# A 16-expert MoE layer with two token sets: the context products issued in runs of four k tiles instead of two

## The chip, the core and the metric

The kernel runs on one core of a Trainium2 chip. A core has TensorE (PE in the profile, with its weight loads shown as PEld), VectorE (DVE), ScalarE (ACT), GpSimd (POOL), SyncE (SP, which here only issues transfers) and sixteen DMA engines. The metric is device time in microseconds; the number quoted for a kernel is the median of several executions. Everything that is read from the trace comes from one further profiled execution, with times counted from the start of its span.

## The reference, cut to what matters

The model has two layers over 1024 latent tokens and 256 context tokens with 1024 channels. Each layer is a token mixer followed by an expert-choice mixture of experts: each of 16 experts picks its own tokens, 128 latent ones and, in layer 0 only, 32 context ones, and applies a gated two-layer network to them.

```python
def _ec_moe(h, router, w1, w3, w2):
    bsz, n_tok, d = h.shape
    cap = EC_CAPACITY * n_tok // N_EXPERTS
    aff = jax.nn.softmax(jnp.einsum('btd,de->bte', h, router).astype(F32), axis=-1)
    gate, idx = lax.top_k(jnp.swapaxes(aff, 1, 2), cap)
    xe = jax.vmap(lambda hb, ib: hb[ib])(h, idx)
    hid = jax.nn.silu(jnp.einsum('becd,edf->becf', xe, w1)) * jnp.einsum('becd,edf->becf', xe, w3)
    ye = jnp.einsum('becf,efd->becd', hid, w2) * gate[..., None].astype(h.dtype)
    ...
for i in range(DEPTH):
    ...
    x_lat = x_lat + mod_l[5] * _ec_moe(...)
    if i < DEPTH - 1:
        x_ctx = x_ctx + mod_c[5] * _ec_moe(...)
```

The weights `w1`, `w3` and `w2` of an expert are 1024 x 1024 each, in 32-bit floats, and both token sets use the same ones.

## The kernel before

`Moe` works through the sixteen experts of a layer. In layer 0 it has two token sets. The three matrices of an expert are cut into eight k tiles of 128 rows each. `tiles` loads two k tiles at a time (1 MB) into a `raw` buffer, of which layer 0 has eight, and makes of each k tile two operands: `uhi`, the value rounded to a short significand, on ACT (line 1184, inside `split_hl`), and `ulo`, the rest, on DVE (line 1185). Layer 0 has six buffers for each of these.

The products of the 128 latent tokens use these operands: for a k tile of a matrix there are three products (high by high, high by low, low by high) with two halves of 512 columns, six matmuls over the whole 128 x 128 array (lines 1573 in `up`, 1624 in `down`). The products of the 32 context tokens use `raw` itself in full 32-bit floats. They use 32 columns of the array, so four of them, for four blocks of columns of the weights, stand side by side in four column groups and write to the four 32-partition bands of one PSUM bank (lines 1579 in `up`, with 512 columns each, and 1630 in `down`, with 256). In the records each of these 32-bit matmuls shows as two MATMUL instructions.

`up` computes the hidden activations from `w1` and `w3`, `down` the output from `w2`. Both collect the k tiles in `raws` and issue the context products of the last `CG` of them in one go, behind the latent products of the last one. This text calls that a run. With `CG = 2` there is a run behind k tiles 1, 3, 5 and 7: four in each `up` and four in each `down`. A run of `up` has 16 MATMUL instructions in the records (two k tiles, four groups, two each), and so has one of `down`.

`run` orders the work: `up` of expert e, halfway through it (behind k tile 3) `turn` of the expert before, which transposes its hidden activations, and `operands` of the next expert, which transposes its gathered rows; then `down` of the expert before. Every engine works through its own instructions in a fixed order, which the tile framework's planner lays down when the program is built; mostly it is the order of the code, with small exchanges.

SP issues the loads of `raw` (line 1512) in order. A load waits until its buffer is free, that is until both splits and the context products of the buffer's earlier content are done. The order of the buffers is: for k tiles 0 and 1 `w1`, then `w3`, and so on, eight loads for an `up`, then four for a `down`.

Layer 1 has no context tokens in its MoE, other buffer counts, and no runs.

Of the kernel before, what the change touches and what calls it, by code (L numbers as in the profile page):

```python
# [17 lines left out]
DRAM = bass.MemoryType.DRAM  # L18

D = 1024  # L20
NCTX = 256
NLAT = 1024
T = NCTX + NLAT
# [8 lines left out]
def step_of(m):  # L32
    """Step at which direction 1 meets chunk m, and the chunk of a step."""
    return 3 - m if m < 4 else 23 - m
# [6 lines left out]
def rows_ap(t, off, rows, cols):  # L41
    """rows x cols view of a contiguous DRAM tensor, from element `off`."""
    return bass.AP(tensor=t.tensor, offset=t.offset + off, ap=[[cols, rows], [1, cols]])
# [12 lines left out]
def log_exp_table(K):  # L56
    """Loads the activation table that serves Ln and Exp together."""
    K.table = K.tc.keep_in_program_order(K.nc.scalar.preload_act_table_set("natural_log_exp_and_others")).ins


def behind(K, ins, name):
    """Keeps an instruction behind the named one in program order."""
    K.tc.add_manual_dep(ins.ins, name, mybir.DependencyInfo(
        mybir.DependencyClass.NoSync, mybir.DependencyReason.DATA), reason="order")


def after_table(K, ins):
    """Keeps an activation behind the last explicit table load."""
    if ins.ins.name not in K.pinned:
        K.pinned.add(ins.ins.name)  # L70
        behind(K, ins, K.table.name)


class Fill:
    """Generators advanced beside a main stream, one slice at a time; lead: instructions they are moved forward."""
# [26 lines left out]
# ---------------------------------------------------------------- constants  # L102
# [4 lines left out]
def consts(K, A):  # L107
# [9 lines left out]
    # per 64-row half: free index minus row index of the half  # L117
# [5 lines left out]
    for h in range(2):  # L123
        r = slice(64 * h, 64 * h + 64)
# [41 lines left out]
    # silu(c), silu(c_ctx) as [128 d, k, 32] stationaries with two live columns  # L166
# [6 lines left out]
# ---------------------------------------------------------------- ada modulation  # L173
def ada_part(K, A, layer, jj, wp, pp, wtag="adaw", ptag="adap", bufs=2):
    """N-chunks 4jj..4jj+3 of layer's modulation rows: rows 32g (lat), 32g+1 (ctx) of modr[:, jj]."""
# [37 lines left out]
def modcol(K, layer, m, kt, s):  # L213
    """[128,1] column of modulation m for channels 128kt.., stream s (0 lat, 1 ctx)."""
# [4 lines left out]
def mod_bcast(K, layer, m, s, dst):  # L219
    """dst [128, D] <- modulation m of stream s on every partition."""  # L220
# [6 lines left out]
def norm_cols(K, pool, layer, norm, ms, mh, tag):  # L227
    """[128, 2, kt, stream]: gain * (1 + scale), shift of a modulated norm; ms, mh: scale and shift modulations."""
# [11 lines left out]
# ---------------------------------------------------------------- layer-0 input: norm, modulate, transpose  # L240
def head(K, A, hp, hh, hl):
    """hh + hl = modulated RMS norm of [ctx; x], channel layout [128, 8, T]."""
# [61 lines left out]
# ---------------------------------------------------------------- layer-0 projection, column tile by column tile  # L304
def both(nc, out, ps, func, **kw):
    """Activation of a projected column tile (context, latent) into token order."""
# [4 lines left out]
class InProj:  # L311
    """Projected column tiles (first column, continuation), weights loaded two tiles ahead across runs."""
# [28 lines left out]
    def run(self, posts, fills, drain):  # L341
        """Continues the next tiles with posts; fills: (generators, slices per k tile); drain: those to finish."""
# [23 lines left out]
def post_z(K, j, wk, tag, bufs):  # L366
    """Stores the silu of gate tile j."""
# [9 lines left out]
# ---------------------------------------------------------------- RWKV-7 operands  # L377
def store_L(K, unit, n0, x, rev=False):
    """x [(half, s), chunk, t] -> K.s_L [unit, chunk, half, s, t]; chunks n0.. (descending if rev)."""
# [3 lines left out]
class Rwkv:  # L383
    """Token shift, loras, decays and the chunk operands alpha, rho, beta, kappa of both directions.

    With c the running sum of the log decay inside a chunk, in the direction's order:
    alpha = kk e^(c-), rho = r e^c, beta = b e^-c, kappa = k e^-c.
    """
# [26 lines left out]
    def shift(self, ps, j, out):  # L415
        """out = (1 - mu) p + mu/2 (previous + next), zero beyond the ends of each stream."""
# [29 lines left out]
    def invert(self, ct):  # L446
        """Queues the inverses of a column tile once its chunk matrices are traced."""
# [5 lines left out]
    def prep_gen(self, ct):  # L453
# [14 lines left out]
        for bi, (a, m) in enumerate(BLK):  # L468
# [75 lines left out]
            # bonus and gate  # L544
# [28 lines left out]
# ---------------------------------------------------------------- gated DeltaNet operands  # L573
class Gdn:
    """Short convolution, gates and the chunk matrices of the gated delta rule, keys and queries not normalised.

    With nk = 1/|k|: L[t,s] = (k_t.k_s) e^(g_t-g_s) nk_s^2 beta_s, A[t,s] = (q_t.k_s) e^(g_t-g_s) nk_s^2 beta_s,
    r = v/nk - e^g S k, Y = (I+L)^-1 r, o = q S e^g + A Y, S' = e^(gl) S + (k nk^2 beta e^(gl-g))^T Y.
    Rows 0-63 carry direction 0, rows 64-127 direction 1 in flipped token order.
    """  # L580
# [12 lines left out]
    def to_chunks(self, ps, src, w):  # L593
        """ps [(d, p), step, w] <- src [128 token, tile, d, w], direction 1 flipped."""
# [20 lines left out]
    def gates(self, ab):  # L615
# [11 lines left out]
        # softplus(x) = max(x, 0) + ln(1 + e^-|x|)  # L627
# [33 lines left out]
    def conv(self, ps, j):  # L661
        """Five-tap centred convolution over tokens of column tile j."""
# [40 lines left out]
    def sums(self, sq, s, h):  # L703
        """K.ssq[tok, tile, s, h] = sum over channels of the squares, plus eps."""
# [23 lines left out]
    def tok(self, x, h, c0, scaled):  # L728
        """Channel tile x -> token rows of K.s_kv [T, 1024], columns of head h (values divided by nk)."""
# [60 lines left out]
# ---------------------------------------------------------------- inverses of the 32-blocks of I + L  # L790
def inv_blocks(K, c0):
    """The tensor of the inverses of chunk c0, its number of chunks and the place of c0 in it."""
# [3 lines left out]
def tri_inv(K, pool, parts, store, bufs=2):  # L796
    """Inverts the two 32-row diagonal blocks of 64x64 chunk matrices, one block per lane.

    parts: (unit, swap, first chunk, chunks), lanes (chunk, half, q) each. K.s_L holds L^T (L where swap is set);
    K.s_T [form, unit, chunk, half, q, 32, 32] receives the inverse (form 0) and its transpose (form 1), chunks  # L800
    of the context and of the latent tokens apart.
    """
# [38 lines left out]
# ---------------------------------------------------------------- the two scans, chunk by chunk  # L841
def scan_rows(K):
    """K.rows: token rows of each step, rows 0-63 forward, rows 64-127 backward; and rows of K.s_o[0 or 1]."""
# [15 lines left out]
class Scan:  # L859
# [14 lines left out]
    def tri_tile(self, n):  # L874
        """Tile of the inverses of step n, its zero blocks set."""
# [9 lines left out]
    # -- loads  # L885
    def load2(self, m):
        """Channel operands of steps 2m, 2m+1."""
# [24 lines left out]
    def load_tri(self, n):  # L912
        """Inverse blocks of step n."""
# [14 lines left out]
    def load_tok(self, n):  # L928
        """Token operands of step n."""
# [14 lines left out]
    # -- matrices that do not wait for the state  # L944
    def gram(self, n):
        """Chunk products of the RWKV operands of step n, and their operands on token rows; six slices."""
# [32 lines left out]
    def corner(self, n):  # L979
        """The off-diagonal 32-block -T22 L21 T11 of every inverse of step n; six slices."""  # L980
# [161 lines left out]
    def run(self, later, tri):  # L1142
        """All steps; later: called with a load of a later step; tri: inverses that only latent steps need."""
# [31 lines left out]
# slices of a step: r and n the two recurrences, g and c the matrices of the next step between them  # L1175
# [5 lines left out]
# ---------------------------------------------------------------- scan outputs -> mixer output, channel layout  # L1181
def split_hl(K, hi, lo, src):
    """hi = src rounded to the short significand, lo = src - hi."""
# [4 lines left out]
def post_rwkv(K, p, ps, mh, ml, ct, a, m, o):  # L1188
    """Generator: loads, mean, variance and the rest."""
# [26 lines left out]
def post_gdn(K, p, ps, mh, ml, tt, o_):  # L1216
    """Generator: the normed rows, then their turn into channel layout."""
# [27 lines left out]
def turns(posts):  # L1245
    """Slices of the generators of a block (one slice in already), a later one between the two of each."""
# [4 lines left out]
def load_split(K, wp, W, rows, cols, name, parts, bufs=3, tag="wstage", gain=None, stage=None, now=True):  # L1251
    """Resident hi/lo [128, rows/128, cols] of a DRAM matrix; parts: (k tile, partition, nrows, row0) pieces.

    gain: factors of the columns, on every partition; with now False the third result is a generator that loads and
    splits, one k tile a slice.
    """
# [26 lines left out]
def tile_rows(t, tt):  # L1283
    """Rows of token tile tt of a (context, latent) pair of DRAM tensors."""
# [3 lines left out]
def load_raw(K, t, W, last):  # L1288
    """t [128, 8, 1024] <- a square matrix, to be split later; issued behind instruction last."""
# [12 lines left out]
def bcast_mods(K, A, layer, s, cpool, tpool, ps, ms, norm, tag, tb=2, shared=None):  # L1302
    """Modulations ms of stream s on every partition; the first one as norm gain * (1 + scale) if norm is given."""
# [20 lines left out]
def out_tile(K, p, op, ps2, ps1, m, wh, wl, tt, x_src, g2, nrm, router, aff, bufs=2, tb=2, t0=0, halves=False):  # L1324
    """Out projection of token tile tt, residual, FFN norm, router affinities of the tile; a generator.

    Slices: eight of the product, then two turns, the router product and the affinities.

    m(k): hi and lo of channel tile k of the branch; halves: the product is made one half of the columns after the
    other, in one bank.  # L1330
    g2: gate of the branch on every partition, or None where the weights carry it. K.s_h holds the normed rows
    before the modulation nrm.
    """
# [1005 lines left out]
```

## Time and profile before

| | |
|---|---|
| median of 3 runs | 3622.27 us (3619.68 to 3623.23) |
| the profiled execution: span from its first to its last instruction | 3620.5 us |
| PE busy | 3343.5 us, 92% of the span |
| DVE busy | 2421.4 us, 67% |
| ACT busy | 2073.4 us, 57% |
| mean granted TensorE clock | 0.943 of full speed |
| MoE of layer 0, in the trace | from about 1540 to 2340 us |

The profiled execution's record holds its span and no time of its own beside it; the span is 1.8 us under the median of the runs. Busy shares are means over all stages of the kernel. A busy PE in these records is one with a matmul in flight. Idle time of an engine is put down to what ended it.

### The profile page before, as it was taken

How to read it: one execution, taken by the hardware profiler on the slowest of the kernel's cores; microseconds unless marked ns; L12 is line 12 of the kernel's file. 1: busy time of each engine (PE TensorE's matmuls, PEld its weight loads, DVE VectorE, ACT ScalarE, POOL GpSimd, SP SyncE). 2: the span in 40 equal slices, each digit the busy share in tenths (PEclk: the TensorE clock that was granted, in tenths of full speed). 3: DMA queues.
4: the chain of work that ended last, by engine and by line, in shares of the span. 5: the costliest groups of instructions: out<-in, count | busy, mean ns of one | idle time of the engine just before them, and what ended most of it. 6: DMA issues, size and time to landing. Idle time of an engine off the chain costs nothing. (4 is left out here: it accounts for less than half of the span.)

```text
span 3620.5 us, 60293 instructions
## 1 busy us (share of the span) xinstructions
PE 3343.5 (92%) x23392; PEld 2475.0 (68%) x23392; DVE 2421.4 (67%) x4034; ACT 2073.4 (57%) x3529; POOL 731.6 (20%) x716
## 2 busy tenths in 40 slices
PE   5999999996999979699999999899899986999997
PEld 3866667775888867566666666567667764888885
DVE  4267774667343356967777777644666588999998
ACT  4244554332333356376666666453577745888886
POOL 1233322222322244111111100101223310101001
PEclk8999999996999989899999999999699997999998
DMA  5255565666897756468888887663311138999995
GB/s 190 70 190 172 183 204 172 225 187 126 172 210 162 162 167 209 152 245 282 282 288 278 284 286 265 202 230 123 77 39 44 47 110 306 378 396 386 394 375 217
DMA packets 480161, 767.80 MB, mean 212 GB/s; under 512 B 231836, under 2 KB 318532, under 8 KB 472708
## 3 DMA queue, kind: packets, MB, share of 16 engines
q1 hardware_dynamic: 434640, 601.05, 50.2%
q0 software_dynamic: 41648, 151.55, 13.5%
q10 hardware_dynamic: 3587, 11.36, 1.0%
q8 instruction: 184, 3.01, 0.3%
q14 instruction: 102, 0.83, 0.1%
HBM read 631.48 MB, written 132.38 MB: 211 GB/s over the span
## 5 line engine op out<-in xcount | busy, mean ns | idle before, releaser
L1185 DVE TENSOR_TENSOR ulo<-raw,uhi 128x1024 fp32r<-128x1024 f32 x768 | 901.6, 1222 | 127.6 <-ACT uhi L1184 118.9
L1184 ACT ACTIVATE uhi<-raw 128x1024 fp32r<-128x1024 f32 x768 | 789.4, 1069 | 245.2 <-PE ps_y L1624 127.0
L1573 PE MATMUL ps_h<-uhi,xh 128*128 128x512 f32 x1024 | 333.7, 404 | 1.4 <-ACT uhi L1184 1.3
L1573 PE MATMUL ps_h<-ulo,xh 128*128 128x512 f32 x1024 | 320.4, 393 | 3.0 <-DVE ulo L1185 1.0
L1573 PE MATMUL ps_h<-uhi,xl 128*128 128x512 f32 x1024 | 319.0, 392 | 0.0
L1640 POOL DMA_INDIRECT s_x<-yo,idxl x31 | 49.2, 1587 | 977.1 <-DVE yo L1636 977.1
L1573 PEld LDWEIGHTS ps_h<-uhi,xh 128*128 128x128 f32 x1024 | 184.0, 188 | 73.5 <-ACT uhi L1184 21.4
L1573 PEld LDWEIGHTS ps_h<-ulo,xh 128*128 128x128 f32 x1024 | 190.6, 188 | 54.9 <-DVE ulo L1185 12.4
L1573 PEld LDWEIGHTS ps_h<-uhi,xl 128*128 128x128 f32 x1024 | 191.2, 188 | 41.5
L354 PE MATMUL ps_in<-hl,whi 128*128 128x512 f32 x512 | 172.2, 411 | 0.0
L354 PE MATMUL ps_in<-hh,wlo 128*128 128x512 f32 x512 | 169.4, 409 | 1.5 <-POOL wlo L338 1.5
L354 PE MATMUL ps_in<-hh,whi 128*128 128x512 f32 x512 | 169.5, 408 | 0.9 <-DVE convu L671 0.9
L1624 PE MATMUL ps_y<-uhi,th 128*128 128x512 f32 x512 | 167.2, 407 | 0.6 <-ACT tc L1610 0.5
L1624 PE MATMUL ps_y<-ulo,th 128*128 128x512 f32 x512 | 161.1, 395 | 0.1
L1624 PE MATMUL ps_y<-uhi,tl 128*128 128x512 f32 x512 | 158.7, 391 | 0.0
L1910 DVE CUSTOM_DVE_ANT_0 pe<-ps_s,amask,sink 128x640 f32<-128x640 f32 (+2 forms) x128 | 104.4, 816 | 66.7 <-PE ps_s L1903 65.0
L966 DVE TENSOR_TENSOR ar<-ps_g,strict 64x256 f32<-64x256 f32 x80 | 33.8, 422 | 154.2 <-PE ps_g L964 153.9
L1923 POOL TENSOR_SCALAR pe<-pe,ast 128x640 f32<-128x640 f32 (+1 forms) x48 | 92.1, 1919 | 215.1 <-DVE ast L1922 193.7
L1546 ACT ACTIVATE xv<-ps_x,Gf 128x128 f32<-128x128 f32 x256 | 96.7, 471 | 66.7 <-PE ps_x L1542 66.7
L1579 PE MATMUL ps_hc<-raw,xc 128*32 128x512 f32 x1024 | 126.1, 599 | 0.0
L1624 PEld LDWEIGHTS ps_y<-uhi,th 128*128 128x128 f32 x512 | 91.1, 188 | 49.7 <-issue 20.1
L1345 PE MATMUL ps_out<-woh,mh 128*128 128x512 f32 x288 | 117.6, 454 | 0.0
(509 smaller groups left out, 7548.9 us busy)
## 6 DMA issues: line engine op xcount, KB each, us to landing
raw<-in_moe_w_dram SPq DMA_DIRECT2D x384, 1024.0 KB
ada_w<-in_ada_w_dram SPq DMA_DIRECT2D x48, 1024.0 KB
wraw<-in_e_w_in_dram SPq DMA_DIRECT2D x32, 512.0 KB
s_rk<-arbk POOLq DMA_DIRECT2D x16, 1024.0 KB, 5.7
kq<-s_kq SPq DMA_DIRECT2D x20, 512.0 KB
s_x<-ox POOLq DMA_DIRECT2D x18, 512.0 KB
s_h<-ot POOLq DMA_DIRECT2D x18, 512.0 KB, 4.1
s_rkv<-rkv POOLq DMA_DIRECT2D x12, 640.0 KB, 3.9
```

The costliest lines, as they stand in the source:

```text
L354: nc.tensor.matmul(ps, l[:, k, :], r[:, k, a:a + m], start=(k == 0 and n == 0), stop=(k == 7 and n == 2))
L966: nc.vector.tensor_mul(ar[orow, hp, :, cd[d]], pg[orow, :, 0:64], K.strict[orow, d:d + 1, :].to_broadcast([64, 4, 64]))
L1184: K.nc.scalar.activation(hi, src, AF.Copy)
L1185: K.nc.vector.tensor_sub(lo, src, hi)
L1345: nc.tensor.matmul(po[:, cp_], l, r[:, k, c_], start=(k == 0 and n == 0), stop=(k == 7 and n == 2))
L1546: nc.scalar.activation(v[:, q], pt[:, q], AF.Identity, bias=self.nrm[:, 1, k, 0:1], scale=self.nrm[:, 0, k, 0:1])
L1573: nc.tensor.matmul(pl[m][n], l[:, k], r[:, 512 * n:512 * n + 512], start=(k == 0 and i == 0), stop=(k == 7 and i == 2))
L1579: nc.tensor.matmul(pc[32 * g:32 * g + 32], xc[:, k_], rs[g // 2][:, 512 * (g % 2):512 * (g % 2) + 512], start=(k_ == 0), stop=(k_ == 7), s ...
L1624: nc.tensor.matmul(py[n], l[:, k], r[:, 512 * n:512 * n + 512], start=(k == 0 and i == 0), stop=(k == 7 and i == 2))
L1640: nc.gpsimd.indirect_dma_start(out=K.s_x[1], out_offset=bass.IndirectOffsetOnAxis(ap=idx[:, e:e + 1], axis=0), in_=yo, in_offset=None, com ...
L1910: nc.vector.tensor_tensor_reduce(pe[:, a:b], sc[:, 512 - nl + a:512 - nl + b], self.mask[:, m:m + b - a], 1.0, low, OP.add, OP.min, st[:, ...
L1923: (nc.vector if n < NV else nc.gpsimd).tensor_scalar(pes[0][:, :nk], pes[0][:, :nk], st[:, 4, 0:1], None, op0=OP.mult)
```

## The change

One constant changes: the number of k tiles whose context products are issued in one run goes from two to four. The same products are issued, on the same operands. The runs behind k tiles 1 and 5 are gone, and those behind k tiles 3 and 7 have 32 MATMUL instructions instead of 16. Buffer counts are the same. The rest of the diff drops comments and docstrings.

```diff
-RAW1, UB1 = 13, 4          # load and split buffers of the layer without context tokens
-CG = 2            # k tiles whose context products run in one go
+RAW1, UB1 = 13, 4
+CG = 4
```

The two places that read it (unchanged):

```python
            if xc is not None and k % CG == CG - 1:      # in up
                for k_, *rs in raws[-CG:]:
...
            if tc_ is not None and k % CG == CG - 1:     # in down
                for k_, raw in raws[-CG:]:
```

## Rows read from the trace of the kernel before

**Rows 1.** The page: span, and TensorE's busy time over the span.
```profile
span 3620.5 us, 60293 instructions
...
PE 3343.5 (92%) x23392; PEld 2475.0 (68%) x23392; DVE 2421.4 (67%) x4034; ACT 2073.4 (57%) x3529; POOL 731.6 (20%) x716
```

**Rows 2.** Windows: length, PE, PEld, DVE, ACT, POOL busy; clock, DMA share, GB/s.
```profile
1540.00:1580.00 40.00, 37.35 (x186) 23.90 (x189) 26.35 (x25) 34.03 (x59) 7.80 (x7) 0.88 0.58 210
1600.00:2300.00 700.00, 700.00 (x4248) 459.57 (x4247) 512.21 (x524) 477.94 (x678) 75.16 (x52) 1.00 0.82 281
2300.00:2340.00 40.00, 37.33 (x257) 22.91 (x255) 24.55 (x30) 17.95 (x20) 4.18 (x3) 1.00 0.39 115
```

**Rows 3.** Groups by line: the context matmuls of `up` and of `down`.
```profile
L1579 PE MATMUL ps_hc<-raw,xc x1024: 592/592/1062, 1547.5 to 2302.3; 128*32 128x512 f32 x171
L1630 PE MATMUL ps_yc<-raw,tc x1024: 379/379/404, 1617.4 to 2337.8; 128*32 128x256 f32 x171
```

**Rows 4.** Timeline of PE around the run behind k tile 5 of an `up`.
```profile
1801.62 0.61 PE L1573 MATMUL ps_h<-uhi,xl 128*128 128x512 f32 x2
1802.17 1.92 PE L1579 MATMUL ps_hc<-raw,xc 128*32 128x512 f32 x16
1804.02 0.74 PE L1573 MATMUL ps_h<-uhi,xh 128*128 128x512 f32 x2
...
1806.92 0.62 PE L1573 MATMUL ps_h<-uhi,xh 128*128 128x512 f32 x2
...
1809.18 0.61 PE L1573 MATMUL ps_h<-uhi,xl 128*128 128x512 f32 x2
```

**Rows 5.** Timeline of PE around the run behind k tile 1 of a `down`.
```profile
1814.02 0.62 PE L1624 MATMUL ps_y<-uhi,tl 128*128 128x512 f32 x2
1814.57 1.07 PE L1630 MATMUL ps_yc<-raw,tc 128*32 128x256 f32 x16
...
1818.01 0.62 PE L1624 MATMUL ps_y<-uhi,tl 128*128 128x512 f32 x2
```

**Rows 6.** Timeline of PE's weight loads inside a run of `up`.
```profile
1791.95 0.13 PEld L1579 LDWEIGHTS ps_hc<-raw,xc 128*32 128x32 f32 x4 [0.30 <-issue]
1792.38 0.13 PEld L1579 LDWEIGHTS ps_hc<-raw,xc 128*32 128x32 f32 x4 [0.30 <-issue]
```

**Rows 7.** Timeline of PE: one run of the first expert's `up`, and what follows.
```profile
1564.27 2.77 PE L1579 MATMUL ps_hc<-raw,xc 128*32 128x512 f32 x22
1566.98 0.73 PE L1573 MATMUL ps_h<-uhi,xh 128*128 128x512 f32 x2
```

**Rows 8.** Waits of SP's queue from 1600 to 2300: total, times, longest.
```profile
SPq L1512 <- PE ps_hc L1579: 428.2, 57, 9.8
SPq L1512 <- PE ps_yc L1630: 189.8, 56, 3.5
```

**Rows 9.** Timeline of SP's queue: three pairs of loads.
```profile
1793.45 0.88 SPq L1512 DMA_DIRECT2D raw<-in_moe_w_dram  x2
...
1804.12 0.88 SPq L1512 DMA_DIRECT2D raw<-in_moe_w_dram  x2
...
1811.68 0.88 SPq L1512 DMA_DIRECT2D raw<-in_moe_w_dram  x2
```

**Rows 10.** Windows of one microsecond; the last number is GB/s.
```profile
1804.00:1805.00 1.00, 1.00 (x8) 0.83 (x5) 1.00 (x2) 1.00 (x2) 0.00 (x0) 1.00 0.00 0
...
1809.00:1810.00 1.00, 1.00 (x8) 0.49 (x10) 0.27 (x1) 1.00 (x2) 0.00 (x0) 1.00 1.00 414
...
1811.00:1812.00 1.00, 1.00 (x10) 0.37 (x3) 1.00 (x2) 0.48 (x2) 0.00 (x0) 1.00 0.02 8
```

**Rows 11.** Timelines of ACT (first, last) and DVE (middle): splits.
```profile
1802.32 5.88 ACT L1184 ACTIVATE uhi<-raw 128x1024 fp32r<-128x1024 f32 x6
...
1803.50 5.77 DVE L1185 TENSOR_TENSOR ulo<-raw,uhi 128x1024 fp32r<-128x1024 f32 x5 [0.79 <-ACT uhi L1184]
...
1817.28 1.06 ACT L1184 ACTIVATE uhi<-raw 128x1024 fp32r<-128x1024 f32 x1 [1.54 <-PE ps_y L1624]
```

## Prediction

> **What bounds the kernel now.** I read the page first: TensorE is busy for 92% of the span, so a change of TensorE's own work can move the end [rows 1]. The windows then say where. In the MoE of layer 0, the only stage with runs, TensorE has a matmul in flight for 700.00 of the 700 us from 1600 to 2300, at the full granted clock, with DVE at 73%, ACT at 68% and the DMA engines at 82% [rows 2]. So in this stage TensorE's stream of matmuls is the bound, and a microsecond taken out of it is a microsecond of the kernel as long as ACT, DVE and the loads keep up. The first 40 us (busy 37.35, clock 0.88) and the last 40 (37.33) are less dense. The timeline of TensorE says what a run costs, SP's waits say what it releases, and the timelines of ACT, DVE and SP say how much cover there is; these follow where they are used.
>
> **What is removed.** The context matmuls stay, 1024 MATMUL instructions in all the `up`s and 1024 in all the `down`s [rows 3]. What goes is the borders of runs: the work of the runs behind k tiles 1 and 5, in each `up` and each `down` of 16 experts, joins a later run, so 16 x 4 = 64 entries and exits fall away.
>
> What entry and exit cost, in an `up`: a pair of latent matmuls at the steady rate takes 2.26 / 5 = 0.452 us (1806.92 to 1809.18, five pairs). From the start of the last pair ahead of the run (1801.62) to the start of the first pair of k tile 7 (1806.92) are 5.30 us. In them are that pair and the six pairs of k tile 6, 7 x 0.452 = 3.16, and the run; so the run takes 2.14 [rows 4]. Inside a run the four groups start a round of four instructions every 0.43 us [rows 6]; 16 instructions are four rounds, 1.72. The other 2.14 - 1.72 = 0.42 us is what a run costs beyond its products: 0.10 ahead of its first matmul (0.55 from the last pair to the run, not 0.45), the rest in its last round's end and in the pairs behind it, which start 0.58 and less apart until the steady rate is back.
>
> In a `down` the same: 1814.02 to 1818.01 is 3.99 us with six pairs, 2.71, so a run takes 1.28 [rows 5]. Its matmuls have 256 columns, so half a round, 0.215 (the two forms' durations differ by 592 - 379 = 213 ns for 256 columns [rows 3]); four make 0.86, and 0.42 is left.
>
> TensorE's sequence repeats from expert to expert, so I take 0.42 for each removed run that stood between latent matmuls. Rounding of the steady pair (0.452 or 0.454) makes it 0.405 to 0.42.
>
> A rule of the Trainium skill bears on the size. "TensorEngine Tiling (Array Packing)", Key Properties, says that a change of tiling mode drains the array; a drain and refill is the fixed part of a lone matmul in "TensorE: Matmul & The Clock Gate", Single matmul latency, 398 cycles at the warm clock, so by estimate 0.17 us, and two switches a run 0.33. By that the sum would be 64 x 0.33 = 21 us; the rows, which hold the slower pairs behind a run too, give more, and the sum goes by them.
>
> **What is added.** The runs that stay have eight rounds instead of four. Whether a longer run costs more than its rounds is shown by the first expert, where the planner has already made one of 22 instructions: 2.71 us from its start to the next matmul (1564.27 to 1566.98), against 1.85 for four rounds; the 0.86 between is two rounds of 0.43, and 22 instructions are five and a half [rows 7]. So a longer run adds nothing.
>
> **Sum.** I don't count the two runs of the first expert's `up`, which stand in the stretch that isn't dense and are cut up and joined otherwise already. 62 x 0.42 = 26.0 us. Bounds: 60 x 0.405 = 24.3 and 64 x 0.42 = 26.9, with nothing lost elsewhere. The profiled execution then has 3620.5 - 26.0 = 3594.5 us, and the median, 1.8 above, 3596.
>
> **What is moved: the release of the load buffers.** SP's loads wait for nothing but context runs: 428.2 us for those of `up`, 189.8 for those of `down` [rows 8]. A load goes into a buffer eight loads after its earlier content, so the pairs at 1793.45, 1804.12 and 1811.68 follow the runs behind k tiles 3, 5 and 7 [rows 9]. After the change k tiles 0 to 3 are given back together and 4 to 7 together: the pair of 1804.12 goes out with that of 1811.68, 7.6 us later, as a burst of four.
>
> How long a burst takes: the pair issued at 1804.12 moves nothing until 1805, goes at 414 GB/s, and is over at 1811.0 (8 GB/s behind it) [rows 10]. That is 6.9 us, of which 2.10 MB / 414 GB/s = 5.1 are data, 2.5 a load, and 1.8 the start. Four take 1.8 + 4 x 2.5 = 11.9 us. Issued at 1811.3 (the run now ends 0.4 earlier), they land at 1815.6, 1818.1, 1820.7 and 1823.2. They are k tiles 0 to 3 of the next `up`. That `up` starts where `down` ends: two k tiles of `down` take 3.99, so 1818.01 + 2 x 3.99 + 0.55 + 1.00 = 1827.5 before [rows 5], and 1826.3 with three borders gone on the way. A split takes 1.06 on ACT and 1.2 on DVE, so the first operand is ready at 1817.9, 8 us ahead; the last two loads are wanted two k tiles (5.4 us) later, 1831.7, and are split by 1825.5, 6 us ahead. In the first case ACT didn't wait for the load before but for a split buffer that TensorE held (1817.28) [rows 11], so most of the delay falls into idle time. I cost the later loads at nothing; what covers them is ACT's lead of six tiles. If a burst came more than 6 us late, each further microsecond would cost 15, once an expert.
>
> **The tightest place.** ACT makes `turn`'s and `operands`' values behind the transposes that follow k tile 3, and only at 1802.32 comes to the splits of k tile 7; six follow back to back, and DVE's five from 1803.50 [rows 11]. DVE has `ulo` of `w1`'s k tile 7 ready at 1803.50 + 1.22 = 1804.7 and that of `w3` 1.15 later. TensorE wanted the first at 1806.92 + 0.45 = 1807.4 [rows 4]. ACT's chain hangs on transposes that stand ahead of the removed run and doesn't move; TensorE comes 2.14 us earlier, at 1805.2. So 0.5 us of cover is left of 2.7 there (0.7 for `w3`). It holds by these rows; each microsecond beyond would cost 14, in the experts that have both a predecessor and a successor.
>
> The PSUM bank that the runs of `up` and `down` share is wanted later after the change (behind k tile 3, not 1), so its readers have more time. The longer pause in which no split buffer is freed, 3.6 instead of 1.9 us, stops ACT and DVE for longer, but eight tiles are 8 x 1.22 = 9.8 us of DVE in 10.9 us of TensorE with six buffers of lead.
>
> **Rivals.**
> *Part of it is lost at k tile 7* (or the planner cuts some of the long runs in two; in the first expert it made pieces of its own [rows 7]). Each microsecond of wait takes 14 of the 26: 3601 to 3615. For it: 0.5 us is a thin cover, and the planner lays the order anew. Against: the sequences repeat to 0.01 us.
> *No change that can be measured.* The waits at k tile 7 eat it all, 26 / 14 = 1.9 us each, or the planner keeps runs as short as they were: 3615 to 3629. A difference within 0.2%, 7 us, is about what a measurement of this kernel can't tell from none.
> *Slower: the burst of four is late.* The loads stand behind each other and beside the gathers; DMA is at 82% over the stage [rows 2], and every microsecond in which no buffer is free is lost to it. A burst of 20.5 us instead of 11.9 would use up the 6 us of cover and make TensorE wait for 2.6 us in each of 15 experts, 39 us against 26: 3635. It decides from 11.9 + 6 + 1.7 = 19.6 us, that is loads of 4.5 us, not 2.5. Against: 12 loads x 2.5 = 30 us of data in a period of about 49.
>
> **How the numbers follow.** Full gain 0.74 (3593 to 3601), part lost 0.12, none 0.08, slower 0.06. Likeliest: 3596. The range leaves out the last two and little of the second: 3591 to 3609. Faster by over 0.2% (under 3615): 0.86; within 0.2%: 0.08; slower: 0.06.
>
> **What would show it.** In the changed kernel's trace: runs of 32 at 3.57 and 1.86 us to the next latent matmul; 64 pauses fewer; the stage from 1600 on shorter by 26 us and still without idle TensorE; pairs of SP's loads become fours, with a longest wait of some 16 us. Wrong would be: TensorE waiting for `ulo` or `uhi` behind k tile 6 of each `up`, for DMA at an `up`'s start, or runs of 16.

## The result, and the profile after

| | before | after |
|---|---|---|
| median of four runs each | 3622.68 us (3619.68 to 3623.23) | 3598.81 us (3584.89 to 3601.77) |
| ratio | | 0.993 (95%: 0.9908 to 0.9952) |
| the profiled execution: time, span | span 3620.5 us | 3600.8 us, span 3599.0 us |

The kernel became 23.9 us faster, 0.7%. The forecast was 3596.0 us with a range of 3591 to 3609. Of the executions further below, three were slow throughout and count in no ratio, though in the medians given: two of the kernel before beside the first experiments (5022.84 and 6262.18 us), and the first profiled one of runs_of_one (3859.86 us, at a mean granted clock of 0.815 in place of 0.94).

The page of the kernel after: TensorE is busy 28 us less than in [rows 1], and the span is 21.5 us shorter.
```profile
span 3599.0 us, 60251 instructions
...
PE 3315.3 (92%) x23392; PEld 2486.7 (69%) x23392; DVE 2414.6 (67%) x4034; ACT 2071.8 (58%) x3529; POOL 732.2 (20%) x716
```

The windows of after, in the order of [rows 2]. In the dense stretch TensorE still has no idle time and its full clock, and puts 4110 matmuls into 650 us (before: 3953 in the same 650 us).
```profile
1540.00:1580.00 40.00, 36.21 (x178) 23.66 (x179) 25.94 (x26) 32.70 (x57) 7.61 (x7) 0.87 0.59 214
1600.00:2250.00 650.00, 650.00 (x4110) 452.15 (x4109) 488.44 (x506) 460.49 (x662) 72.30 (x51) 1.00 0.81 292
2272.00:2312.00 40.00, 39.37 (x284) 26.18 (x282) 25.23 (x28) 18.96 (x22) 3.18 (x3) 1.00 0.47 154
```

The groups of the context matmuls answer to [rows 3]: the same count and the same duration of one.
```profile
L1579 PE MATMUL ps_hc<-raw,xc x1024: 592/592/1062, 1549.1 to 2278.5; 128*32 128x512 f32 x171
...
L1630 PE MATMUL ps_yc<-raw,tc x1024: 379/379/404, 1620.6 to 2311.7; 128*32 128x256 f32 x171
```

The timeline of TensorE around the run behind k tile 7 of an `up` and the first run of the `down` behind it (before: [rows 4, 5]). The first two lines are the transposes with which `turn` begins for two successive experts; the next two lead from latent products into the transposes of `operands`.
```profile
1739.78 0.98 PE L1602 MATMUL ps_t<-ident,hid 128*128 128x128 f32 x7
...
1787.34 1.09 PE L1602 MATMUL ps_t<-ident,hid 128*128 128x128 f32 x8
...
1789.32 0.62 PE L1573 MATMUL ps_h<-ulo,xh 128*128 128x512 f32 x2
1789.78 1.03 PE L1542 MATMUL ps_x<-ident,xe 128*128 128x128 f32 x8
...
1801.05 0.61 PE L1573 MATMUL ps_h<-uhi,xl 128*128 128x512 f32 x2
1801.60 3.64 PE L1579 MATMUL ps_hc<-raw,xc 128*32 128x512 f32 x32
1805.17 0.73 PE L1624 MATMUL ps_y<-uhi,th 128*128 128x512 f32 x2
1805.74 0.62 PE L1624 MATMUL ps_y<-ulo,th 128*128 128x512 f32 x2
1806.20 0.62 PE L1624 MATMUL ps_y<-uhi,tl 128*128 128x512 f32 x2
...
1810.83 1.93 PE L1630 MATMUL ps_yc<-raw,tc 128*32 128x256 f32 x32
1812.70 0.73 PE L1624 MATMUL ps_y<-uhi,th 128*128 128x512 f32 x2
```
A run of `up` takes 1805.17 - 1801.60 = 3.57 us to the next latent matmul, one of `down` 1812.70 - 1810.83 = 1.87. The first two pairs behind a run take 0.57 and 0.46 us, a little less than in the kernel before (0.58 and 0.47).

Two measures are used from here on, both read from the trace. The **period** is the time from one expert's first `turn` transpose to the next one's: above, 1787.34 - 1739.78 = 47.56 us. Before it was 1793.35 - 1744.05 = 49.30:
```profile
1744.05 1.09 PE L1602 MATMUL ps_t<-ident,hid 128*128 128x128 f32 x8
...
1793.35 1.09 PE L1602 MATMUL ps_t<-ident,hid 128*128 128x128 f32 x8
```
Every steady period of a kernel with runs of one length is the same to 0.04 us. The **stage** is the time from the first split of the first expert to the end of the last context matmul: 768.35 us, and 795.57 before, 27.2 less. Both are sharper than a kernel's whole time: a second profile of the same changed kernel (below) gave 768.29.

What is not this stage: the stage began 1.1 us later than before, and the attention of layer 1, which the change doesn't touch, took 420.3 us instead of 415.7. So the span of this profile got -27.2 + 1.1 + 4.6 = -21.5 us.

SP's waits from 1600 to 2250, and the issues of the four loads for the next `up`'s k tiles 0 to 3 (before: [rows 8, 9]).
```profile
SPq L1512 <- PE ps_hc L1579: 395.7, 53, 15.2
SPq L1512 <- PE ps_yc L1630: 176.3, 55, 6.2
```
```profile
1803.55 0.88 SPq L1512 DMA_DIRECT2D raw<-in_moe_w_dram  x2
...
1805.27 0.92 SPq L1512 DMA_DIRECT2D raw<-in_moe_w_dram  x2
```
The pairs have become fours, with a longest wait of 15.2 us. The four don't go out at once: the long run gives the buffers back while it goes on, the first pair 1.7 us before the second.

The tight place: ACT's and DVE's splits of k tile 7 (the timelines of the two engines), and the pairs of TensorE that want `ulo`.
```profile
1796.32 3.98 ACT L1184 ACTIVATE uhi<-raw 128x1024 fp32r<-128x1024 f32 x4
...
1797.49 3.50 DVE L1185 TENSOR_TENSOR ulo<-raw,uhi 128x1024 fp32r<-128x1024 f32 x3 [0.79 <-ACT uhi L1184]
...
1799.24 0.62 PE L1573 MATMUL ps_h<-ulo,xh 128*128 128x512 f32 x2
...
1800.60 0.62 PE L1573 MATMUL ps_h<-ulo,xh 128*128 128x512 f32 x2
```
DVE needs 1.22 us for one, so the first `ulo` is ready at 1798.71, 0.53 us before TensorE wants it at 1799.24; that of `w3` has 0.75.

ACT's waits from 1600 to 2250, the row for late loads: five microseconds in all, none of which reached TensorE.
```profile
ACT uhi L1184 <- DMA raw<-in_moe_w_dram: 5.1, 9, 1.2
```

### The profile page after: what moved, and what is told of

It is laid out like the page before. It is cut to its first block, busy times and chain, and to the rows that moved or that the text cites. A ratio compares the mean times of both kernels' runs of the same rounds, so it can differ in the third digit from the quotient of the medians.

```text
span 3599.0 us, 60251 instructions
## 1 busy us (share of the span) xinstructions
PE 3315.3 (92%) x23392; PEld 2486.7 (69%) x23392; DVE 2414.6 (67%) x4034; ACT 2071.8 (58%) x3529; POOL 732.2 (20%) x716
```

## Experiments

Two theories stood against each other at first. The *border theory* is the prediction's: each border of a run (its entry and exit together) costs TensorE the same, 0.42 us by the prediction, and the number of borders is all that matters. The *load theory* says that the later and larger bursts of loads are the gain. The two are tied together in the change, since fewer borders come with later release. The third question was what the thin cover at k tile 7 is worth.

Where a ratio is given, the whole time is a median, and the ratio is to the kernel before on the same chip (median 3622.73 us for late2, runs_of_one, up_only and down_only; 3604.31 for after_again, up4_down8 and eight). The other whole times are of one execution each.

What a border is made of can be read from the starts of single matmuls. In the kernel before, a latent matmul takes 0.227 us to the next one at the steady rate, but 0.318 to the first matmul of a run; the first of a run's rounds takes 0.02 and the last 0.11 more than the others; the eleven latent matmuls behind hold 0.17 more than the steady rate. Together that is 0.40 us. What makes the entry dear is the step from the whole array to a part of it, not the type of the values: the transposes of `operands` use full 32-bit floats too, but the whole array, and the last pair ahead of them takes 1789.78 - 1789.32 = 0.46 us, the last pair ahead of a run 1801.60 - 1801.05 = 0.55 (both in the changed kernel's timeline above).

**1. Late release, all the borders (late2).** The runs stay at two k tiles, but the first two k tiles of four wait and go shortly before the others, two pairs of latent matmuls apart in `down`.
```diff
+                if tc_ is not None and i == 0 and k % 4 == 3:
+                    ctx_run(raws[-3:-1])       # the first two k tiles of the four
...
-            if tc_ is not None and k % CG == CG - 1:
-                for k_, raw in raws[-CG:]:
+            if tc_ is not None and k % 4 == 3:
+                ctx_run(raws[-2:])
```
(the same in `up`)

> As the changed kernel, but the long run behind k tile 3 (and 7) is cut in two by latent products: two k tiles' context products stand inside k tile 3, two behind it. So there are as many runs as before the change, and the load buffers are given back late, nearly as after it. The stage means the MoE of layer 0 from its first weight split on ScalarE to the end of its last context matmul: 795.6 us before, 768.4 after. If the borders of runs are what was saved: stage 793 to 797, total within 5 us of before. If the saving came from the loads, which go out in bursts of four: stage about 768 and total near 3599.

Measured: 3620.73 us, ratio 1.0 (0.9987 to 1.0014); period 49.07, stage 791.5. Eight runs of 16 an expert as before, SP's longest wait 13.8 us, almost that of after, and no gain in the whole time. The load theory falls. The lines of two successive experts' first transposes, for the period, and then the timeline of a `down`, for the small rest of 0.23 us an expert:
```profile
1741.64 1.09 PE L1605 MATMUL ps_t<-ident,hid 128*128 128x128 f32 x8
...
1790.70 1.09 PE L1605 MATMUL ps_t<-ident,hid 128*128 128x128 f32 x8
```
```profile
1813.67 1.07 PE L1628 MATMUL ps_yc<-raw,tc 128*32 128x256 f32 x16
1814.67 0.74 PE L1634 MATMUL ps_y<-ulo,th 128*128 128x512 f32 x2
1815.25 0.63 PE L1634 MATMUL ps_y<-uhi,tl 128*128 128x512 f32 x2
1815.82 1.07 PE L1628 MATMUL ps_yc<-raw,tc 128*32 128x256 f32 x16
```
Behind a run several pairs are slower than the steady 0.453 us, the first by 0.13 and the next ones by 0.01 each. Where the next run follows two or three pairs later, 0.02 to 0.03 us of that falls away; and behind the second of two such runs the latent matmuls hold 0.13 us beyond the steady rate, not 0.17. Over an expert's four such couples of runs that makes the 0.23. Why the pairs behind a second run are faster was not tried.

**2. More borders (runs_of_one, runs_of_one_again).** Runs of one k tile everywhere.
```diff
-CG = 4
+CGU, CGD = 1, 1     # read in up, in down
```

> A run behind each k tile, twice the runs of before: 8 for each up and down, 128 more in all. If each border costs 0.41 us whatever the length of the run: stage 795.6 + 128 x 0.41 = 848, total about 3675 (the kernel gives buffers back a little earlier, which by itself brings nothing as TensorE is the bound). If the cost is not in the borders but in how buffers come free: stage near 795.

Measured: 3667.88 us, ratio 1.0111 (1.0081 to 1.0141), slower by 1.1%, some 40 us. The stage is taken from a second profile, at the usual clock:

> Runs of one k tile throughout, once more for a profile at the usual clock. Border theory: eight more borders an expert than before at 0.42 to 0.435 us, less what eight instructions of slower pairs that the shorter stretch cuts off would save: period 52.6 to 52.8 us against 49.30, stage 844 to 851 us. Rival (the gain is from the later, larger loads and not from the borders): stage within 5 us of 795.6.

Measured: period 51.69, stage 834.2, 38.6 more than before; one execution of 3634.03 us beside one of 3603.03 of before. The direction is that of the border theory; the size is under the expectation (52.6 to 52.8, 844 to 851). One reason is in the trace: there are 15 runs an expert, not 16, since the planner joined two of `down`'s. So seven more borders cost 2.39 us, 0.34 each, not the 0.42 and more that was expected. The starts of the matmuls say where the rest is: the runs themselves hold 0.14 us beyond their rounds in both kernels, but the latent matmuls behind a run hold 0.14 to 0.17 us beyond the steady rate here and 0.17 before, so that most of the fifteen borders are somewhat cheaper. A border's price is not quite a constant.

**3. Half the change (up_only, down_only).** Runs of four in `up` alone and in `down` alone.
```diff
-CG = 4
+CGU, CGD = 4, 2     # up_only; 2, 4 in down_only
```

> Runs of four k tiles in up alone, of two in down. 32 borders fewer than before, two of them in the first expert: stage 795.6 - 31 x 0.42 = 782.6, total about 3609. If the saving were that of down's runs alone, or if it needed both, stage 795 or more.

> Runs of four k tiles in down alone, of two in up. 32 borders fewer: stage 795.6 - 32 x 0.42 = 782.2, total about 3609. The two single parts add up to the whole if borders are independent: 13 + 13.5 against 27.2.

Measured: `up_only` 3609.49 us, ratio 0.9982 (0.9964 to 0.9999), period 48.45, stage 783.1; `down_only` 3606.21 us, ratio 0.9958 (0.9941 to 0.9975), period 48.41, stage 781.0. The gains in the stage, 12.5 and 14.6, add up to the whole's 27.2 to 0.2 us. Both halves save two borders an expert, 0.43 and 0.45 us each (49.30 - 48.45 = 0.85, 49.30 - 48.41 = 0.89); so the 512-column and the 256-column runs have the same border to 0.02 us. The two times don't show the halves as evenly as the stage does: the attention behind them took 416.0 us in one profile and 423.2 in the other.

**4. The same kernel again (after_again), and longer runs (up4_down8, eight).**
```diff
-CG = 4
+CGU, CGD = 4, 8     # up4_down8; 8, 8 in eight
```

> The changed kernel once more, to see which part of it repeats. The stage (MoE of layer 0, first split to last context matmul) should again be 768.3 to 768.5 us; the attention of layer 1, from the last matmul of its input projection to its last output matmul, took 415.7 us in the profile of before and 420.3 in that of after. If that is scatter of the executions, it comes out anywhere between 414 and 424 here; if the change caused it, at 420 again.

> Runs of four k tiles in up, of eight in down (one behind k tile 7). One border less an expert: stage 768.4 - 16 x 0.41 = 761.8, total 6 or 7 us under the changed kernel. The four loads that down holds until its end are those of the next up's k tiles 4 to 7, wanted 14 us later, and a burst of four takes 11.9, so no wait is expected. If it is late all the same: stage 768 or more, with TensorE or ScalarE waiting for the load.

> Runs of eight k tiles in both, one behind each up and down. Borders alone: two less an expert than the changed kernel, period 47.56 - 0.82 = 46.7 us, stage 755. But all eight load buffers are then held until up's long run; down's first load is issued some 1.8 us into the run, lands 4.3 us later and is split 2.3 us after that, 8.4 us after the run's start, where TensorE wants it at 7.7: a wait of 0.7 to 1.2 us an expert, stage 766 to 773, with the gain given back at the start of down. Loads of no consequence: 755. Loads later than worked out: over 775.

Measured, all on one chip: the changed kernel again 3572.86 us, ratio 0.9914 (0.9901 to 0.9928), stage 768.3; `up4_down8` 3566.1, ratio 0.9902 (0.9887 to 0.9918), stage 767.1; `eight` 3622.55, ratio 1.0063 (1.0043 to 1.0084), stage 811.1.

`up4_down8` has one border less an expert; at 0.43 us its period would be 47.13. The periods go from 47.17 to 48.23, with a mean of 47.51. The undisturbed ones are 47.17 to 47.20, so this border, between two runs of four k tiles, was worth 0.36. In the others the loads become late. ACT's waits for them from 1580 to 2210, TensorE's row in the same window, and then the timelines of ACT and TensorE in an expert of 48.0 us:
```profile
ACT uhi L1184 <- DMA raw<-in_moe_w_dram: 67.3, 47, 3.7
```
```profile
1580.00:2210.00 630.00, 628.39 (x3970) 439.62 (x3969) 479.53 (x493) 444.77 (x638) 69.60 (x48) 1.00 0.81 290
```
```profile
1758.20 1.06 ACT L1184 ACTIVATE uhi<-raw 128x1024 fp32r<-128x1024 f32 x1 [2.82 <-DMA raw<-in_moe_w_dram]
1760.72 1.06 ACT L1184 ACTIVATE uhi<-raw 128x1024 fp32r<-128x1024 f32 x1 [1.46 <-DMA raw<-in_moe_w_dram]
1761.68 1.06 ACT L1184 ACTIVATE th<-ps_t 128x512 fp32r<-128x512 f32 x2
1762.63 0.38 ACT L1610 ACTIVATE tc<-ps_tc 128x256 f32<-128x256 f32 x1
```
```profile
1763.07 1.39 PE L1542 MATMUL ps_x<-ident,xe 128*128 128x128 f32 x8 [0.31 <-ACT tc L1610]
```
Not the split that was late stops TensorE, but what stands behind it on ACT: `turn`'s values `th` and `tc` come after the two waits, and the next transposes want the bank that ACT reads; they start late and take 1.39 us, 1.03 in the changed kernel. All that the periods have beyond 47.20 lies in this place, 4.4 us over the fourteen. It ate most of the expected 6.6 us. The whole time is 6.8 us under that of the changed kernel on the same chip, of which the stage explains 1.2, and the intervals of the two ratios overlap: it is not shown to be faster.

`eight` goes to the other side, as the prediction's third rival had it for four, and much further than the 766 to 773 us that were expected. ACT's waits and TensorE's window from 1600 to 2250, and TensorE between an `up` and a `down`:
```profile
ACT uhi L1184 <- DMA raw<-in_moe_w_dram: 86.7, 50, 7.4
```
```profile
1600.00:2250.00 650.00, 638.51 (x3862) 429.58 (x3862) 464.39 (x480) 426.97 (x624) 73.65 (x48) 0.99 0.76 278
```
```profile
1794.16 7.08 PE L1579 MATMUL ps_hc<-raw,xc 128*32 128x512 f32 x64
1802.19 0.73 PE L1624 MATMUL ps_y<-uhi,th 128*128 128x512 f32 x2 [0.95 <-ACT uhi L1184]
```
With all of an `up`'s buffers given back together at its end, the first load of the next matrices is late and TensorE stands still. The planner also ordered the experts quite differently (periods of some 24 and 76 us in turn, more and shorter pieces of runs: 87 in the stage, 69 in the changed kernel). TensorE's idle time, 11.5 us of the 650, is the smaller part of the 43 us over the changed kernel's stage; how much of the rest the pieces cost was not measured by itself.

**5. The cover at k tile 7 (act_late2, act_late2_cg2, act_late1).** Spare copies on ACT ahead of its splits, in the changed kernel and in the one before.
```diff
+            for _ in range(2):      # range(1) in act_late1; CG = 2 in act_late2_cg2
+                nc.scalar.activation(x, x, AF.Copy)
```

> The changed kernel with two spare copies of 128x1024 on ScalarE at the end of operands in layer 0 (of rows that nobody reads any more), one ahead of each split of the next k tile 7. If half a microsecond of cover is all that is left there, 0.53 for w1 and 0.75 for w3 in the trace: first copy 0.95 late, wait 0.42; second 1.9 late, wait 0.73 more; 1.15 us in each of 14 experts, stage 768.4 + 16 = 784. If ScalarE has slack there: 768.

> The kernel before (runs of two k tiles) with the same two spare copies on ACT behind operands' values that act_late2 has; they overwrite x with itself and change no product. Theory (tight place at k tile 7): before, the splits of that k tile are 2.65 and 2.87 us ahead of TensorE, so 0.95 us more on ACT stays inside the cover: steady period 49.3 us as in the kernel before, stage 795.6 us, within 1 us. Rival (copies on ACT there cost TensorE their time whatever the cover, for instance through the transposes): period 50.3 to 50.9, stage 810 to 817.

> The changed kernel with one spare copy on ACT behind operands' values instead of two (it overwrites x with itself and changes no product). Theory (tight place at k tile 7, 0.53 us of cover left): one copy takes some 0.95/2 to 0.95 us; if it takes about 0.95 the wait is 0.4 us, period 48.0 and stage 774.3; if it takes about 0.48 it stays inside the cover, period 47.56 to 47.6 and stage 768.3 to 769. Either way under half of act_late2's 14.7 us. Rival (the copies cost by their number): half of act_late2's, stage 775.7, period 48.35.

Measured, one execution each (3593.42, 3601.95 and 3588.56 us, the first on another chip than the other two): `act_late2` has a period of 49.14, 1.58 more than the changed kernel; the control on runs of two 49.30, as without copies; `act_late1` 48.74, 1.18 more. The stages are 783.0, 789.2 and 777.7 us, but here they mislead: in all three the first `turn` was placed some 7 us earlier (its transposes begin 46 to 47 us into the stage, not 53.4), so that a stage with copies is shorter by that. The stage of `act_late2` met its number only for that reason, the periods are what counts, and `act_late1` lies well above the 48.0 that was expected at the most, and above its rival's 48.35.

So the cover is real: with 2.65 us of it two copies cost nothing (1.71 are then left), with 0.53 they cost 1.58 us an expert. But the price isn't a wait. TensorE is without idle time in `act_late1` and in `act_late2`; `act_late2`'s window, and its timeline behind the latent pairs of k tile 6 (lines are two further down than in the changed kernel):
```profile
1600.00:2250.00 650.00, 650.00 (x3974) 436.88 (x3973) 477.79 (x494) 465.43 (x658) 73.35 (x50) 1.00 0.80 283
```
```profile
1778.78 1.05 PE L1581 MATMUL ps_hc<-raw,xc 128*32 128x512 f32 x2
1779.76 0.73 PE L1575 MATMUL ps_h<-uhi,xh 128*128 128x512 f32 x2
...
1781.80 1.06 PE L1581 MATMUL ps_hc<-raw,xc 128*32 128x512 f32 x8
1782.80 0.73 PE L1575 MATMUL ps_h<-ulo,xh 128*128 128x512 f32 x2
...
1783.92 2.77 PE L1581 MATMUL ps_hc<-raw,xc 128*32 128x512 f32 x22
```
The run of 32 is cut into 2 + 8 + 22: where the operand is late, context matmuls have been put forward, and each piece has its border. That the planner does it to fill the time is argued from the place, not shown. In `act_late1` it is 2 + 30:
```profile
1778.28 1.05 PE L1581 MATMUL ps_hc<-raw,xc 128*32 128x512 f32 x2
1779.26 0.73 PE L1575 MATMUL ps_h<-uhi,xh 128*128 128x512 f32 x2
...
1782.21 3.63 PE L1581 MATMUL ps_hc<-raw,xc 128*32 128x512 f32 x30
1785.77 0.73 PE L1626 MATMUL ps_y<-uhi,th 128*128 128x512 f32 x2
```
A piece of two takes 0.98 us to the next latent matmul, as much as a piece of eight (1.00): two rounds, whether one group is at work in them or four. The 30 that are left take 3.56 us, no less than 32 (3.57). So `act_late1` pays two rounds, 0.86 us, and a border for the remaining 0.32. The second piece of `act_late2` takes its two rounds out of the last one (22 take 2.71) and adds a border alone, 1.58 - 1.18 = 0.40. That is more than the lateness itself: in `act_late1` `ulo` of `w1` is ready 0.76 us before it is wanted, and the piece holds TensorE up by 0.98, so without it TensorE would have waited for 0.2 us by this estimate. In `act_late2` that of `w3` is ready 1.34 us ahead with pieces of 0.98 and 1.00: by estimate 0.6 us of waiting, against 1.58 paid.

## Why the prediction was right

**The border of a run: right, and a little small.** The term was 0.42 us a border. The period fell by 49.30 - 47.56 = 1.74 us for four borders, 0.435 each; up_only's and down_only's two gave 0.43 and 0.45. The number of them was right too: the context matmuls stand in 69 pieces in the stage, 131 before, 62 fewer. Counted over the stage, 27.2 us stand against the predicted 26.0 and above the upper bound of 26.9: steady periods 14 x 1.74 = 24.4, the last period 1.3 (32.45 to 31.14), the last expert's end 1.4, the first part 0.1.

The prediction's one price hides two. A border that goes takes 0.40 us with it, a little under the term, and three of the four borders that stay become 0.04 cheaper, which the prediction did not foresee. The 24 latent matmuls between two runs show it: 1809.73 - 1804.02 = 5.71 us before ([rows 4] have the first time, the line below the second), 1810.83 - 1805.17 = 5.66 after. 4 x 0.40 and 3 x 0.04 are the 1.7 us of the period. Why the pairs are faster behind a longer run was not tried.
```profile
1809.73 1.92 PE L1579 MATMUL ps_hc<-raw,xc 128*32 128x512 f32 x16
```
The prediction's estimate of 21 us from two pages of the Trainium skill, "TensorEngine Tiling (Array Packing)", Key Properties, and "TensorE: Matmul & The Clock Gate", Single matmul latency, was too low. The trace agrees that each step between the whole array and a part of it has a price (0.09 us going in, 0.11 coming back); the estimate has no term for the slower pairs behind a run, 0.17 of the 0.40.

**Longer runs add nothing: right.** 3.57 and 1.87 us were read where 3.57 and 1.86 were foretold, and every steady run has 32 instructions, none cut. They even save the 0.04 us behind them.

**The release of the buffers: right for four, and the limit is near.** Loads go out in fours, the longest wait is 15.2 us (some 16 was said), and ACT waited 5.1 us in all without cost to TensorE. That the late release is neither gain nor loss is shown by late2. Only the burst was not one: it is spread over 1.7 us. With eight k tiles in `down`, and above all in both, the rival of late loads comes true.

**The tightest place: right in size, wrong in what it would do.** 0.53 and 0.75 us of cover were left, where 0.5 and 0.7 were foretold. The prediction priced a lack of cover as waiting of TensorE; with one or two copies on ACT the planner cut the run instead, which the rival named only in brackets, and in act_late1 that cost more than the wait would have. In the changed kernel itself no steady run was cut.

**What the numbers missed.** The sum gave a span of 3594.5 us, and 3599.0 came. The stage was 1.2 us better than the sum; 1.1 us before it and 4.6 in the attention went the other way. The attention took between 412 and 423 us in the profiles at the usual clock, all of kernels whose code for it is the same, 420.3 and 419.3 in the two profiles of the changed kernel, and 415.2 with `up4_down8`. Why it differs was not tried; that the changed kernel's two profiles agree to 1 us leaves open that the 4.6 us belong to the changed program and are no scatter. The changed kernel gained 31.4 us by the medians when it was run again, on another chip, and 23.9 the first time; the stage's 27.2 lies between. So the stage bears out the mechanism, and that the median came within 3 us of the forecast is in part luck.

## What to carry to other kernels

Where TensorE changes between its whole array and column groups, count the changes and price one from the timeline, from the last pair ahead to the pair at which the steady rate is back, not only the gap that is seen. Grouping is worth that price times the changes saved until buffers are held too long, and that can come as a wait on an engine that has something else to do behind the late load (ACT in `up4_down8`), before it comes where the load is used (`eight`). Before thinning a cover, look at what the planner does when it runs out: matmuls that it puts into the gap can cost more than the gap.

## What the runs showed that was not expected

One context matmul alone in its column group holds TensorE as long as four beside each other (0.98 and 1.00 us with the border), and taking it out of its four saves nothing there. So a cut through a group of four costs two rounds beside the border.

The kernel before had a median of 3622.73 us on the first chip and of 3604.31 on the second, 0.5% apart, while the periods of kernels with the same runs agree to 0.01 us wherever they ran. At least a good part of the difference lies ahead of this stage: it starts at 1541 to 1542 us in the profiles of late2, up_only and down_only on the first chip, and at 1518 to 1525 in the four profiles on the second.
